# Softmax weights times values as plain float32 on two column halves, in a two-block transformer on one core

## The chip, the cores and the metric

The program runs on one core of one Trainium2 chip. Its engines run side by side and are held together by semaphores: TensorE (PE in the rows; its weight loads are PEld), VectorE (DVE), ScalarE (ACT), GpSimd (POOL) and SyncE (SP), which here issues the DMAs. The metric is the device time of one execution in microseconds, lower is better. The kernel before has a median of 2799.71 us over 3 runs (2798.59 to 2801.4). The profiled execution took 2796.16 us, and its span, from the first recorded instruction to the last, is 2794.4 us at a mean granted TensorE clock of 0.982 of full speed.

## The reference, cut to what matters

Two layers of one block and two layers of a second block follow one another on a sequence of 256 tokens of width 1024, in float32. Three places multiply softmax weights with values, and only these are changed. In the first block there are two attention branches, with 8 heads of value width 64 each: grouped (2 key/value heads shared by 4 query heads each) and latent (8 value heads of their own). The sequence x looks at 512 keys, the context sequence c at its own 256, and c is only computed in the first of the two layers:

```
def block(qi):
    s = jnp.einsum("bqkgd,btkd->bkgqt", qi, k).astype(jnp.float32)
    w = jax.nn.softmax(s, axis=-1).astype(v.dtype)
    return jnp.einsum("bkgqt,btkd->bqkgd", w, v)
```

In the second block a sparse attention with 8 heads in 2 groups adds three products of weights and values for each head: over 15 compressed blocks, over selected blocks and over a window. With 256 tokens the selected blocks and the window take in all earlier keys.

```
o_cmp = jnp.einsum('bghqc,bcgd->bqghd', p_cmp.astype(v_cmp.dtype), v_cmp)
o_slc = jnp.einsum('bghqk,bgqkd->bqghd', p_s.astype(vs.dtype), ...)
o_win = jnp.einsum('bghqk,bkgd->bqghd', p_w.astype(vwc.dtype), vwc)
```

All the rest (projections, a Fourier branch, gates, MLPs, gated linear attention, norms) is the same before and after.

## The kernel before, in words

Matrix products keep float32 accuracy by splitting each operand into a high and a low part of a shorter type (float32r, `F32R` in the code): h is a rounded copy written by ScalarE, l is the rest, subtracted by VectorE (`split`, L183 and L189). `mm3` (L196) then issues three matmuls, h·h, h·l and l·h. This holds for the streamed weights (`wr` is the raw tile, `wh` and `wl` the parts), for activations (tiles S and H) and, before the change, for softmax weights and values too. Transposes (`tr`, L201) and a few small products run in plain float32.

Attention goes unit by unit, a unit being one head and one tile of 128 queries. A unit has three steps. `scores` multiplies queries and keys into the PSUM tile `sc`, takes the row maximum (`Vcm`, VectorE), the exponential with its row sum (`ea`, ScalarE), the reciprocal and the product by it (VectorE). `turn` transposes the weights on TensorE into PSUM tile `tp`, 128 keys at a time, and splits them into `eh` and `el`. `apply` multiplies them with the values into another `tp` tile: for each 128 keys three matmuls with 64 value columns as the stationary operand and 128 queries moving, so that only 64 of the array's 128 columns are in use; the result, 64 rows by 128 queries, is split into the output activation (S).

The values are held as h and l pairs: `vg` (grouped, tiles H), `V` (latent, tiles S, made by `build_v`), `vsw` (sparse, H) and, for the compressed branch, `cmp["v"]` and the weights `eTc` (H).

`pipe` runs the steps of neighbouring units in turn: scores of unit n, turn of unit n-1, apply of unit n-2. `mix` puts other matrix products (gate and branch projections, modulation, gated linear attention's projections) between these steps: each step yields its estimated TensorE time, and for each such amount times a ratio (`RATIO`, 1.5, 1.2 and so on by stage) it draws steps of the other work; what is left of that runs behind. The framework then schedules each engine's instructions by a simulated timeline within the program's dependencies, and its buffers have fixed counts (`eh` and `el` 2 each, `ea` 3, PSUM `mm` 3, `sc` 2, `tp` 3). All weight DMAs go out from SyncE.

The three stages in the profiled execution: grouped and latent attention of the first layer from about 185 to 530 us, of the second from about 1030 to 1190 us, sparse attention from about 1690 to 1830 us and from about 2375 to 2510 us.

Of the kernel before, what the change touches and what calls it, by code (L numbers as in the profile page):

```python
# [21 lines left out]
P = 128  # L22
D = 1024
S = 256
# [3 lines left out]
BIG = 3e38  # L28
ALPHA = (2.0 * L) ** 0.25
# [119 lines left out]
class Builder:  # L149
# [543 lines left out]
    def attend(self, pairs, nk, vs, h, out, c0):  # L693
# [5 lines left out]
        st = {}  # L699

        def scores():
            sc = self.pt("sc")
            prs = pairs()
# [6 lines left out]
            e = st["e"] = self.t("ea", [P, nk])  # L710
# [5 lines left out]
        def turn():  # L716
            tp = self.pt("tp", [P, kt, P])
            for a in range(kt):
                self.tr(tp[:, a], st["e"][:, a * P:(a + 1) * P])
            st["w"] = [self.t("eh", [P, kt, P], F32R), self.t("el", [P, kt, P], F32R)]  # L720
            yield cost(kt, P)
            self.split(tp, *st["w"])

        def apply():
            eh, el = st["w"]
            po = self.pt("tp")
            for a in range(kt):
                self.mm3(po[:64, :P], vs(a), (eh[:, a], el[:, a]), a == 0, a == kt - 1)
            yield 0.056 * 3 * kt
            oh, ol = out.at(h // 2, c0, P)  # L730
            b = slice(64 * (h % 2), 64 * (h % 2) + 64)
            self.split(po[:64, :P], oh[b], ol[b])
        return scores, turn, apply

    def first_layer(self, l, X, hT, done):
# [21 lines left out]
        vg = [self.t("H", [P, 4, P], F32R) for _ in range(2)]  # L757
# [21 lines left out]
        def ev_kg(i, ps):  # L779
# [3 lines left out]
            self.split(ps[:, P:2 * P], vg[0][:, kt], vg[1][:, kt])  # L783
# [91 lines left out]
        def grouped(s, h, t):  # L875
            g, j = divmod(h, 4)
            gs = slice(64 * g, 64 * g + 64)
            nk = nkeys(s)
            return self.attend(lambda: [(qg[s][g][:, j, t * P:(t + 1) * P], k[:, :nk]) for k in kgT[g]], nk,
                               lambda a: (vg[0][:, a, gs], vg[1][:, a, gs]), h, OT["g"], OFF[s] + t * P)  # L880

        gqa = self.pipe([load_dft] + [fourier(s, g) for s in full for g in range(4)] +
                        [grouped(s, h, t) for s in full for h in range(8) for t in range(2)])
# [74 lines left out]
        def build_v(p):  # L958
            wv = self.load_w(A["w_uv"][l][:, p * P:(p + 2) * P], 2, 2 * P)
            V[p] = V[p + 1] = [self.t("S", [P, 4, 2 * P], F32R) for _ in range(2)]  # L960
            for a in range(0, 4, 2):
# [6 lines left out]
                self.split(ps, V[p][0][:, a:a + 2], V[p][1][:, a:a + 2])  # L968
# [32 lines left out]
        def latent(s, p, i, t):  # L1001
            nk = nkeys(s)
            c = (p % 2) * P + 64 * i
            def pairs():
# [3 lines left out]
            return self.attend(pairs, nk, lambda a: (V[p][0][:, a, c:c + 64], V[p][1][:, a, c:c + 64]),  # L1008
                               2 * p + i, OT["m"], OFF[s] + t * P)

        steps = [partial(build_v, 0), partial(build_k, 0)] + [partial(build_q, s, 0) for s in full]
        for p in range(4):
            for s in full:
                units = [latent(s, p, i, t) for i in range(2) for t in range(2)]
# [236 lines left out]
    def mix2(self, x, st, l, nxt):  # L1251
# [8 lines left out]
        vsw = [self.t("H", [P, 2, 2, P], F32R) for _ in range(2)]  # L1260
# [24 lines left out]
        def ev_kv2(i, ps):  # L1285
            self.split(ps[:, 0:P], vsw[0][:, i, 0], vsw[1][:, i, 0], scale=r[i])
            key_rows(ps[:, P:2 * P], i, 1)
            self.split(ps[:, 2 * P:3 * P], vsw[0][:, i, 1], vsw[1][:, i, 1], scale=r[i])
# [129 lines left out]
    def compress(self, l, kc, name, cmp):  # L1418
# [48 lines left out]
        else:  # L1467
# [18 lines left out]
            o = [self.t("H", [P, 2, 4, 64], F32R) for _ in range(2)]  # L1486
            self.split(z, *o)
        cmp[name] = o

    def nsa(self, qT, ksw, vsw, ga, cmp, OA):  # L1490
# [3 lines left out]
        eTc = [self.t("H", [P, 2, S], F32R) for _ in range(2)]  # L1494
# [37 lines left out]
        self.split(tp, *eTc)  # L1532
        yield cost(8, P)

        def unit(h, t):
            g, j = divmod(h, 4)
            gs = slice(64 * g, 64 * g + 64)
            o = slice(64 * (h % 2), 64 * (h % 2) + 64)
            nk = P * (t + 1)
            n = 2 * (t + 1)  # L1540
            st = {}

            def scores():
                sc = self.pt("sc", [P, 2, 256])
                j0 = 128 - 128 * t
                self.mm2(sc[:, :, :nk], qT[g][:, j // 2, j % 2, t * P:(t + 1) * P], [k[:, :, :nk] for k in ksw[g]])
# [4 lines left out]
                e = st["e"] = self.t("ea", [P, 2, nk])  # L1551
                for b in range(2):
                    nc.vector.tensor_tensor_reduce(e[:, b], sc[:, b, :nk], self.bias[g][:, j, j0:j0 + nk], -1.0, BIG,
# [7 lines left out]
                nc.vector.tensor_tensor(a_, a_, g3[:, h, 1:3], op=ALU.mult)  # L1561
# [3 lines left out]
            def turn():  # L1565
                tp = self.pt("tp", [P, 4, P])
                for a in range(n):
                    b, k = divmod(a, t + 1)
                    self.tr(tp[:, a], st["e"][:, b, k * P:(k + 1) * P])
                st["w"] = [self.t("eh", [P, n, P], F32R), self.t("el", [P, n, P], F32R)]  # L1570
                yield cost(n, P)
                self.split(tp[:, :n], *st["w"])

            def apply():
                eh, el = st["w"]
                ts = slice(t * P, (t + 1) * P)
                po = self.pt("tp")
                out = po[:64, :P]
                self.mm3(out, (cmp["v"][0][:, g, j], cmp["v"][1][:, g, j]),
                         (eTc[0][:, g, ts], eTc[1][:, g, ts]), True, False)  # L1580
# [3 lines left out]
                yield 0.056 * 3 * (n + 1)  # L1584
                oh, ol = OA.at(h // 2, t * P, P)
                self.split(out, oh[o], ol[o])
            return scores, turn, apply
# [223 lines left out]
```

## Time and profile before

| | |
|---|---|
| median of 3 runs | 2799.71 us |
| profiled execution | 2796.16 us |
| its span | 2794.4 us |
| granted TensorE clock, mean | 0.982 |
| PE busy | 2700.5 us, 97% of the span |
| PEld busy | 2377.2 us, 85% |
| DVE busy | 1925.0 us, 69% |
| ACT busy | 1479.7 us, 53% |
| POOL busy | 167.4 us, 6% |

How to read it: an engine's busy time is the union of its records. TensorE's matmuls are pipelined, and a record lasts from its start to its modelled end, so records overlap and their length is not what each costs; the cost of one is read from the distance between the starts of neighbours. In the chain of work that ended last PE holds 75% of the span, and "issue" (time in which the engine waited for nothing that the profile shows) another 15%.

### The profile page before, as it was taken

What the parts mean: (1) busy time and instruction counts of PE and PEld (TensorE: products, weight loads), DVE (VectorE), ACT (ScalarE), POOL (GpSimd) and SP (SyncE); (2) the same over time, 40 slices, a digit from 0 to 9 for tenths busy, and PEclk for the clock granted to TensorE, in tenths of its full rate; (3) what the DMA queues carried; (4) which work ended last, traced back from release to release, by engine and by line L of the source; (5) the groups of instructions that cost most, each with busy time, mean ns of one, the idle gap of its engine ahead of it and who ended that gap; (6) DMA issues with size and microseconds to landing.
All of it is one profiled execution on the core that took longest, in us unless ns stands there. A gap on an engine that the chain in (4) does not pass through costs nothing.

```text
span 2794.4 us, 45721 instructions
## 1 busy us (share of the span) xinstructions
PE 2700.5 (97%) x17359; PEld 2377.2 (85%) x17359; DVE 1925.0 (69%) x3754; ACT 1479.7 (53%) x2970; POOL 167.4 (6%) x304
## 2 busy tenths in 40 slices
PE   8999999999999999979989999999999998999998
PEld 4868878788777799968979987999999988889997
DVE  5676776587886788866675567867656656787664
ACT  6474564453344666655454456645444446665543
POOL 1200010100000210010000001100000000020000
PEclk9999999999999999989999999999999999999999
DMA  7251232465554333346555555446666655436664
GB/s 233 80 166 43 79 114 85 153 216 159 162 184 140 112 108 104 113 145 217 190 188 169 194 158 171 125 142 188 183 189 190 184 181 172 142 94 191 183 185 151
DMA packets 258610, 431.97 MB, mean 155 GB/s; under 512 B 18020, under 2 KB 89100, under 8 KB 258390
## 3 DMA queue, kind: packets, MB, share of 16 engines
q1 hardware_dynamic: 258390, 429.05, 49.6%
q8 instruction: 136, 2.23, 0.3%
q14 instruction: 84, 0.69, 0.1%
HBM read 425.75 MB, written 3.24 MB: 154 GB/s over the span
## 4 chain that ended last, share of the span: by engine, by line
PE 75%; issue 15%; DVE 4%; ACT 2%; DMA 2%; POOL 1%; SPq 0%; DVEq 0%; POOLq 0%; ACTq 0%
PE mm L196 62%; PE tp L196 3%; PE sc L196 3%; PE tp L201 3%; PE sc L705 2%; DVE wl L189 1%; DMA wr<-w_ada 1%; ACT wh L183 1%; PE sc L207 0%; DMA wr<-w_in 0%; DMA wr<-w_o 0%; ACT H L567 0%; POOL Var L233 0%; DVE S L629 0%; DVE S L214 0%
## 5 line engine op out<-in xcount | busy, mean ns | idle before, releaser
L196 PE MATMUL mm<-S,wh 128*128 128x256 f32 (+1 forms) x6112 | 1255.3, 303 | 3.6 <-ACT wh L183 1.3
L189 DVE TENSOR_TENSOR wl<-wr,wh 128x512 fp32r<-128x512 f32 (+2 forms) x1256 | 886.7, 739 | 499.5 <-ACT wh L183 494.8
L183 ACT ACTIVATE wh<-wr 128x512 fp32r<-128x512 f32 (+2 forms) x1256 | 780.1, 662 | 748.5 <-PE mm L196 385.1
L196 PEld LDWEIGHTS mm<-S,wh 128*128 128x128 f32 x6112 | 987.3, 191 | 51.5 <-ACT wh L183 2.8
L196 PE MATMUL mm<-S,wl 128*128 128x256 f32 (+1 forms) x3056 | 918.5, 303 | 2.0 <-DVE wl L189 2.0
L196 PE MATMUL mm<-wh,S 128*128 128x512 f32 (+4 forms) x2592 | 775.5, 378 | 11.7 <-ACT S L183 4.0
L196 PEld LDWEIGHTS mm<-S,wl 128*128 128x128 f32 x3056 | 583.1, 191 | 25.5 <-DVE wl L189 3.9
L196 PEld LDWEIGHTS mm<-wh,S 128*128 128x128 f32 x2592 | 478.5, 190 | 100.0 <-issue 7.0
L196 PE MATMUL mm<-wl,S 128*128 128x512 f32 (+4 forms) x1296 | 487.9, 377 | 0.4 <-DVE wl L189 0.4
L196 PEld LDWEIGHTS mm<-wl,S 128*128 128x128 f32 x1296 | 245.7, 190 | 42.6 <-DVE wl L189 1.2
L201 PE MATMUL tp<-cst,ea 128*128 128x128 f32 x632 | 103.9, 286 | 19.3 <-ACT ea L578 11.1
L495 DVE SCALAR_TENSOR_TENSOR H<-wr,cs,H 128x512 f32<-128x512 f32 x168 | 116.1, 747 | 0.0
L201 PEld LDWEIGHTS tp<-cst,ea 128*128 128x128 f32 x632 | 77.5, 146 | 32.4 <-ACT ea L578 13.0
L183 ACT ACTIVATE eh<-tp 128x512 fp32r<-128x512 f32 (+1 forms) x128 | 65.8, 515 | 58.4 <-PE tp L201 57.7
L189 DVE TENSOR_TENSOR el<-tp,eh 128x512 fp32r<-128x512 f32 (+1 forms) x128 | 74.7, 584 | 30.6 <-ACT eh L183 29.1
L196 PE MATMUL mm<-H,S 128*128 128x512 f32 x384 | 94.2, 392 | 0.3 <-DVE H L189 0.3
L183 ACT ACTIVATE S<-tp 64x128 fp32r<-64x128 f32 (+2 forms) x178 | 60.1, 344 | 58.7 <-PE tp L196 48.7
L196 PEld LDWEIGHTS mm<-H,S 128*128 128x128 f32 x384 | 71.5, 188 | 16.6 <-DVE S L629 0.9
L189 DVE TENSOR_TENSOR S<-tp,S 64x128 fp32r<-64x128 f32 (+2 forms) x178 | 66.3, 376 | 26.3 <-ACT S L183 23.7
L711 ACT ACTIVATE ea<-sc,Vcm 128x512 f32<-128x512 f32 (+1 forms) x96 | 59.0, 615 | 34.5 <-DVE Vcm L708 34.0
L183 ACT ACTIVATE S<-H 128x512 fp32r<-128x512 f32 x106 | 65.2, 621 | 12.4 <-DVE H L934 4.9
L708 DVE TENSOR_REDUCE Vcm<-sc 128x1 f32<-128x512 f32 (+1 forms) x96 | 56.8, 596 | 20.2 <-PE sc L705 19.4
(328 smaller groups left out, 2697.8 us busy)
## 6 DMA issues: line engine op xcount, KB each, us to landing
wr<-w_in SPq DMA_DIRECT2D x160, 512.0 KB
wr<-w SPq DMA_DIRECT2D x116, 512.0 KB
wr<-w_ada SPq DMA_DIRECT2D x96, 512.0 KB
wr<-ffn_w_gate SPq DMA_DIRECT2D x88, 512.0 KB
wr<-ffn_w_down SPq DMA_DIRECT2D x88, 512.0 KB
wr<-ffn_w_up SPq DMA_DIRECT2D x84, 512.0 KB
wr<-w_branch_gla SPq DMA_DIRECT2D x16, 512.0 KB
wr<-w_out SPq DMA_DIRECT2D x16, 512.0 KB
```

The source lines that it names most:

```text
L183: nc.scalar.activation(h, src, AF.Copy, scale=1.0 if scale is None else scale)
L189: (nc.gpsimd if le == "p" else nc.vector).tensor_tensor(l, src, h.bitcast(F32), op=ALU.subtract)
L196: self.nc.tensor.matmul(out, a[i], b[j], start=first and n == 0, stop=last and n == 2, skip_group_check=skip)
L201: self.nc.tensor.transpose(out, in_, self.ident[:n, :n])
L495: nc.vector.scalar_tensor_tensor(acc[j], raw[:, k], c, acc[j], op0=ALU.mult, op1=ALU.add)
L705: nc.tensor.matmul(sc[:, :nk], a, b, start=n == 0, stop=n == len(prs) - 1)
L708: nc.vector.tensor_reduce(nm, sc[:, :nk], axis=AX.X, op=ALU.max, negate=True)
L711: nc.scalar.activation(e, sc[:, :nk], AF.Exp, bias=nm, scale=1.0, accum_out=sm)
```

## The change

Softmax weights and values are no longer split in the three places. The values (`vg`, `V`, `vsw`, `cmp["v"]`) and the transposed weights (`ws`, `eTc`) are single float32 tiles, each written by one ScalarE copy. Two heads are handled together: the unit list now alternates between head 0 of a pair (scores, turn) and head 1 of the pair (scores, turn, apply), and `apply` serves both heads. It calls the new `col2`, which for each 128 keys issues one plain float32 matmul for head 0 into PSUM partitions 0 to 63 (columns 0 to 63 of the array) and one for head 1 into partitions 64 to 127 (columns 64 to 127). The result of both heads, 128 rows by 128 queries, is split once. Head 0's weights lie in the tiles `eh`, head 1's in `el`. `mix` is told 0.24 (`COL2`) for each pair of matmuls, where it was told 0.056 for each of the six before. In all 1344 matmuls of the split kind become 448 plain ones, in 224 pairs.

```diff
+COL2 = 0.24
...
+    def col2(self, out, terms, cost_):
+        for n, (a, b) in enumerate(terms):
+            for i in range(2):
+                self.nc.tensor.matmul(out[64 * i:64 * i + 64], a[i], b[i], start=n == 0, stop=n == len(terms) - 1,
+                                      tile_position=(0, 64 * i))
+        yield len(terms) * cost_
...
-        def turn():
+        def turn(i):
             tp = self.pt("tp", [P, kt, P])
             for a in range(kt):
-                self.tr(tp[:, a], st["e"][:, a * P:(a + 1) * P])
-            st["w"] = [self.t("eh", [P, kt, P], F32R), self.t("el", [P, kt, P], F32R)]
+                self.tr(tp[:, a], es[i][:, a * P:(a + 1) * P])
+            ws[i] = self.t(("eh", "el")[i], [P, kt, P])
             yield cost(kt, P)
-            self.split(tp, *st["w"])
+            nc.scalar.activation(ws[i], tp, AF.Copy)
 
         def apply():
-            eh, el = st["w"]
-            po = self.pt("tp")
-            for a in range(kt):
-                self.mm3(po[:64, :P], vs(a), (eh[:, a], el[:, a]), a == 0, a == kt - 1)
-            yield 0.056 * 3 * kt
-            oh, ol = out.at(h // 2, c0, P)
-            b = slice(64 * (h % 2), 64 * (h % 2) + 64)
-            self.split(po[:64, :P], oh[b], ol[b])
-        return scores, turn, apply
+            po = self.pt("tp")[:, :P]
+            yield from self.col2(po, [([vs(i, a) for i in range(2)], [ws[i][:, a] for i in range(2)])
+                                      for a in range(kt)], COL2)
+            oh, ol = out.at(hp, c0, P)
+            self.split(po, oh, ol)
+        return [(partial(scores, 0), partial(turn, 0)), (partial(scores, 1), partial(turn, 1), apply)]
...
-            self.split(ps[:, P:2 * P], vg[0][:, kt], vg[1][:, kt])
+            nc.scalar.activation(vg[:, kt], ps[:, P:2 * P], AF.Copy)
...
-                self.split(ps, V[p][0][:, a:a + 2], V[p][1][:, a:a + 2])
+                nc.scalar.activation(V[p][:, a:a + 2], ps, AF.Copy)
...
-            self.split(ps[:, 0:P], vsw[0][:, i, 0], vsw[1][:, i, 0], scale=r[i])
+            nc.scalar.activation(vsw[:, i, 0], ps[:, 0:P], AF.Copy, scale=r[i])
...
-        self.split(tp, *eTc)
+        nc.scalar.activation(eTc, tp, AF.Copy)
...
+                terms = [([cmp["v"][:, g, j + i] for i in range(2)], [eTc[:, g, t * P:(t + 1) * P]] * 2)]
                 for a in range(n):
                     b, k = divmod(a, t + 1)
-                    self.mm3(out, (vsw[0][:, k, b, gs], vsw[1][:, k, b, gs]), (eh[:, a], el[:, a]), False, a == n - 1)
+                    terms.append(([vsw[:, k, b, gs]] * 2, [ws[i][:, a] for i in range(2)]))
+                yield from self.col2(po, terms, COL2)
```

The instruction order on TensorE, in the grouped attention of the first layer, where the second `apply` of the stage begins. Before (`mm` rows are a gate projection of the other work, `H_502` and `H_503` the high and low part of the values, `eh` and `el` those of the weights):

```order
L196 MATMUL mm_2178<-S_96,wh_2297 128x512
L196 MATMUL mm_2178<-S_95,wl_2298 128x512
L196 MATMUL mm_2178<-S_97,wh_2297 128x512
L196 MATMUL tp_2042<-eh_2003,H_502 64x128
L196 MATMUL tp_2042<-el_2004,H_502 64x128
L196 MATMUL tp_2042<-eh_2003,H_503 64x128
```

The three last rows come four times in a row, once for each 128 keys. Now, at the same place (`eh` holds the weights of head 0, `el` those of head 1, `H_502` the values in one part):

```order
L197 MATMUL mm_2142<-S_95,wl_2234 128x512
L202 MATMUL tp_2088<-cst,ea_2033 128x128 x4
L699 MATMUL tp_2095<-eh_2014,H_502 64x128
L197 MATMUL mm_2143<-S_91,wh_2146 128x512
L197 MATMUL mm_2143<-S_92,wh_2146 128x512
L699 MATMUL tp_2095<-el_2043,H_502 64x128
```

Three rows for each 128 keys of one head have become two rows for both heads. Here two rows of other work have come between the two heads of the first pair; in the whole program the 448 matmuls stand in 81 uninterrupted runs in 64 PSUM tiles, before the 1344 stood in 131 runs in 128 tiles.

On VectorE, in the same stage, before (`el` is the low part of the weights, the output S is split for one head, 64 rows, at a time):

```order
L189 TENSOR_TENSOR S_1303<-tp_2212,S_1302 64x128
L189 TENSOR_TENSOR el_2244<-tp_2238,eh_2243 128x512
L189 TENSOR_TENSOR S_1303<-tp_2247,S_1302 64x128
L708 TENSOR_REDUCE Vcm_2332<-sc_2329 128x1
L189 TENSOR_TENSOR wl_2759<-wr_2756,wh_2758 128x1024
L708 TENSOR_REDUCE Vcm_2367<-sc_2364 128x1
L189 TENSOR_TENSOR el_2279<-tp_2273,eh_2278 128x512
```

And now:

```order
L190 TENSOR_TENSOR S_1298<-tp_2095,S_1297 128x128
L718 TENSOR_REDUCE Vcm_2127<-sc_2124 128x1
L723 RECIPROCAL Vcr_2132<-Vcs_2129 128x1
L724 TENSOR_SCALAR ea_2130<-ea_2130,Vcr_2132 128x512
L718 TENSOR_REDUCE Vcm_2189<-sc_2186 128x1
L190 TENSOR_TENSOR wl_2520<-wr_2517,wh_2519 128x1024
```

The rows that write `el` are gone, and one row writes the output of both heads.

## Rows read from the trace of the kernel before

**Rows 1.** The page: span, and busy time, share and instructions of PE

```profile
span 2794.4 us, 45721 instructions
...
PE 2700.5 (97%) x17359; PEld 2377.2 (85%) x17359; DVE 1925.0 (69%) x3754; ACT 1479.7 (53%) x2970; POOL 167.4 (6%) x304
```

**Rows 2.** Busy time by stretch: stretch, length, engines, clock, DMA share

```profile
core 0: us, PE busy (x) PEld busy (x) DVE busy (x) ACT busy (x) POOL busy (x), PEclk, DMA share, GB/s
...
185.00:325.00 140.00, 140.00 (x944) 120.74 (x943) 92.79 (x224) 74.97 (x182) 3.66 (x2) 1.00 0.20 57
...
1030.00:1190.00 160.00, 159.15 (x1428) 153.49 (x1427) 129.47 (x290) 102.60 (x241) 6.32 (x4) 1.00 0.35 105
...
1690.00:1830.00 140.00, 131.31 (x940) 118.09 (x940) 111.80 (x293) 86.59 (x210) 22.18 (x37) 0.94 0.44 131
```

**Rows 3.** Waits of PE, 1030:1190: who waited for whom, us, times, longest

```profile
PE tp L196 <- DVE el L189: 0.5, 1, 0.5
```

**Rows 4.** Groups of PE by form: operation, shapes, count | busy, mean ns

```profile
L196 PE MATMUL tp<-eh,H 128*64 128x128 f32 x512 | 61.5, 227 | 0.0
L196 PE MATMUL tp<-el,H 128*64 128x128 f32 x256 | 50.0, 224 | 0.0
L196 PE MATMUL tp<-eh,S 128*64 128x128 f32 x320 | 38.8, 229 | 0.1
...
L196 PE MATMUL tp<-el,S 128*64 128x128 f32 x160 | 31.2, 224 | 0.6 <-DVE el L189 0.6
...
L196 PE MATMUL tp<-H,H 128*64 128x128 f32 x96 | 12.4, 239 | 0.0
```

**Rows 5.** Timeline of PE, one apply of 12 matmuls: start, length, instruction

```profile
1061.04 0.22 PE L196 MATMUL tp<-eh,H 128*64 128x128 f32 x1
1061.10 0.22 PE L196 MATMUL tp<-el,H 128*64 128x128 f32 x1
...
1061.71 0.23 PE L196 MATMUL tp<-eh,H 128*64 128x128 f32 x1
1061.78 0.45 PE L196 MATMUL mm<-S,wh 128*128 128x256 f32 x2
```

**Rows 6.** The group of weight loads of 64 columns, by form

```profile
L196 PEld LDWEIGHTS tp<-eh,H 128*64 128x64 f32 x512 | 53.6, 137 | 0.6
```

**Rows 7.** Timeline, plain float32 of 512 columns moving: loads, then matmuls

```profile
529.00 0.09 PEld L527 LDWEIGHTS sc<-wr,cs 128*4 128x4 f32 x1 [0.34 <-issue]
529.43 0.09 PEld L527 LDWEIGHTS sc<-wr,cs 128*4 128x4 f32 x1 [0.34 <-issue]
...
528.57 3.60 PE L527 MATMUL sc<-wr,cs 128*4 128x512 f32 x8
532.10 5.76 PE L196 MATMUL mm<-H,S 128*128 128x512 f32 x24
```

**Rows 8.** Timeline of PE, plain float32 of 128 columns moving

```profile
1785.12 0.60 PE L1626 MATMUL sc<-cst,S 128*128 128x128 f32 x4
1785.48 0.42 PE L196 MATMUL tp<-H,H 128*64 128x128 f32 x3
1785.74 0.23 PE L196 MATMUL tp<-eh,H 128*64 128x128 f32 x1
```

**Rows 9.** The group of PE for that line, by form

```profile
L1626 PE MATMUL sc<-cst,S 128*128 128x128 f32 x32 | 5.0, 277 | 0.0
```

**Rows 10.** Groups of DVE by form: work of the weights' and outputs' split

```profile
L189 DVE TENSOR_TENSOR el<-tp,eh 128x512 fp32r<-128x512 f32 x80 | 54.7, 685 | 18.5 <-ACT eh L183 18.1
...
L189 DVE TENSOR_TENSOR S<-tp,S 64x128 fp32r<-64x128 f32 x128 | 35.9, 280 | 20.2 <-ACT S L183 17.7
...
L189 DVE TENSOR_TENSOR el<-tp,eh 128x256 fp32r<-128x256 f32 x48 | 20.0, 417 | 12.1 <-ACT eh L183 11.1
```

**Rows 11.** The ACT group of the outputs' split, by form

```profile
L183 ACT ACTIVATE S<-tp 64x128 fp32r<-64x128 f32 x128 | 34.4, 269 | 45.8 <-PE tp L196 43.9
```

More of the change, by code (lines that the diff above doesn't have):

```diff
@@ L756, in first_layer @@
         kgT = [[self.t("H", [P, 512], F32R) for _ in range(2)] for _ in range(2)]
-        vg = [self.t("H", [P, 4, P], F32R) for _ in range(2)]
+        vg = self.t("H", [P, 4, P])
         gkv = self.col("mla_kv_g", l)
@@ L1013, in first_layer @@
             for s in full:
-                units = [latent(s, p, i, t) for i in range(2) for t in range(2)]
+                units = [u for t in range(2) for u in latent(s, p, t)]
                 if p < 3:
@@ L1259, in mix2 @@
         ksw = [[self.t("H", [P, 2, S], F32R) for _ in range(2)] for _ in range(2)]
-        vsw = [self.t("H", [P, 2, 2, P], F32R) for _ in range(2)]
+        vsw = self.t("H", [P, 2, 2, P])
         ga = [None, None]
@@ L1485, in compress @@
                 nc.vector.tensor_copy(z[s_, :, a_], ps[s_, :P].rearrange("p (g d) -> p g d", g=2))
-            o = [self.t("H", [P, 2, 4, 64], F32R) for _ in range(2)]
-            self.split(z, *o)
+            o = z
         cmp[name] = o
@@ L1491, in nsa @@
         nc = self.nc
-        eTc = [self.t("H", [P, 2, S], F32R) for _ in range(2)]
+        eTc = self.t("H", [P, 2, S])
         raw = self.pt("tp", [P, 2, 2, P])
@@ L1568, in turn @@
                     b, k = divmod(a, t + 1)
-                    self.tr(tp[:, a], st["e"][:, b, k * P:(k + 1) * P])
-                st["w"] = [self.t("eh", [P, n, P], F32R), self.t("el", [P, n, P], F32R)]
+                    self.tr(tp[:, a], es[i][:, b, k * P:(k + 1) * P])
+                ws[i] = self.t(("eh", "el")[i], [P, n, P])
                 yield cost(n, P)
-                self.split(tp[:, :n], *st["w"])
+                nc.scalar.activation(ws[i], tp[:, :n], AF.Copy)
             def apply():
[L1575 to L1580, printed above, removed]
+                po = self.pt("tp")[:, :P]
+                terms = [([cmp["v"][:, g, j + i] for i in range(2)], [eTc[:, g, t * P:(t + 1) * P]] * 2)]
                 for a in range(n):
                     b, k = divmod(a, t + 1)
-                    self.mm3(out, (vsw[0][:, k, b, gs], vsw[1][:, k, b, gs]), (eh[:, a], el[:, a]), False, a == n - 1)
[L1584 to L1587, printed above, removed]
-        yield from self.pipe([unit(h, t) for h in range(8) for t in range(2)])
+                    terms.append(([vsw[:, k, b, gs]] * 2, [ws[i][:, a] for i in range(2)]))
+                yield from self.col2(po, terms, COL2)
+                oh, ol = OA.at(hp, t * P, P)
+                self.split(po, oh, ol)
+            return [(partial(scores, 0), partial(turn, 0)), (partial(scores, 1), partial(turn, 1), apply)]
+        yield from self.pipe([u for hp in range(4) for t in range(2) for u in units(hp, t)])
     def decays(self, l, alr, la):
```

52 lines of the change are left out of this document (25 added, 27 removed).

## The prediction

> **What bounds the kernel now.** I read the page first: PE is busy for 97% of the span and VectorE for 69% [rows 1]. That is a mean over stages, so I next read the busy time by stretch, at the three places that the change touches. In the first layer's attention PE is busy for all of 140 us, and VectorE for 92.79 of them; in the second layer's for 159.15 of 160, VectorE for 129.47; in the sparse attention for 131.31 of 140, VectorE for 111.80 [rows 2]. Then the waits: in the second layer's attention TensorE waited once for `el`, the low part of the weights, and that for 0.5 us [rows 3]. So in these stages TensorE's own work sets the time, and what counts is what the changed matmuls cost there. VectorE's and ScalarE's work lies beside it.
>
> **What is removed on TensorE.** The groups by form give 512, 256, 320, 160 and 96 matmuls of 64 stationary columns and 128 moving ones [rows 4], 1344 in all, three for each 128 keys of a head. Their mean of some 225 ns is no price, since records overlap. The timeline has twelve of them from 1061.04 to 1061.78, where the next product starts [rows 5]: 0.74 us, or 0.0617 us each, with the load of each one's weights included. That load's record is 137 ns long [rows 6], so loads are already hidden behind the matmuls before them. Removed: 1344 x 0.0617 = 82.9 us.
>
> **What is added on TensorE.** 448 plain float32 matmuls of 64 stationary and 128 moving columns, in 224 pairs. No plain one of 64 columns stands in the trace of before, so I price it by two others. The line of the 128 x 128 running sums, L1626, is reached 16 times (four heads, two tiles, two layers) and has 32 rows [rows 9]: a plain float32 matmul makes two rows. With 512 columns moving, the loads between such rows lie 0.43 us apart, and only the first 0.09 us of that is the load [rows 7]; a quarter of the columns makes 0.43 / 4 = 0.1075 us for a row of 128. The running sums agree: four rows and three matmuls of the split kind take from 1785.12 to 1785.74 [rows 8], and (0.62 - 3 x 0.0617) / 4 = 0.109. So one plain matmul costs 0.215 us, and a pair costs 0.43 us if the two run one behind the other, against 6 x 0.0617 = 0.37 us for the six that it replaces.
>
> All depends, then, on whether the two halves of the columns work at the same time, which nothing in the trace of before shows. Bounds: one behind the other, 448 x 0.215 = 96.3 us, which is 13.4 us more than was removed; wholly side by side, 224 x 0.215 = 48.2 us, or 34.7 us less. I take the case between them that follows if matmuls start in the order in which they stand, as all rows of the timeline do: head 0's second row then runs beside head 1's first, head 1's second beside the first of head 0's next matmul, and a run of n pairs lasts 2n + 1 rows, because in its first and its last row only one half has work. The matmuls stand in 81 runs, so 448 + 81 = 529 rows x 0.1075 = 56.9 us. TensorE gains 82.9 - 56.9 = 26.0 us. For the loads: a pair needs four of 64 columns, and before such a load came every 0.0617 us with a matmul, so four take at most 0.25 us, which is about what the pair takes anyway (56.9 / 224 = 0.254). They don't change the sum, but they leave no reserve.
>
> The Trainium skill, on its page TensorE: Matmul & The Clock Gate, section Measured speedup vs the span model, reports 2.38 times for three tiles side by side in the columns. An estimate from it for two tiles, at the same efficiency, is 1.59 times: 96.3 / 1.59 = 60.6 us, by which the sum would be 22 us instead of 26. No run so far shows it here.
>
> **What goes on VectorE and ScalarE.** The subtractions for `el` take 54.7 + 20.0 us [rows 10] and go; of the 128 output splits half stay, with twice the partitions and the same row length, which saves half of 35.9 us on VectorE [rows 10] and half of 34.4 on ScalarE [rows 11]. That is 92.7 us off VectorE and 17.2 off ScalarE, beside a few rows for the values. I count them at nothing: where TensorE is busy all the time, it hides them already. Bounds: nothing lost, since the engines only get lighter; at most what TensorE idles in these stages, and that is 8.7 us in the first sparse stretch [rows 2] and next to none in the other two. Most of the sparse idle time stands before the units begin, where only the copy of `eTc` gets shorter, so I take 0. `apply` still waits for one ScalarE copy, no longer for a subtraction behind it; behind a waiting `apply` on TensorE stand the next products of other work, as before. What `mix` puts between the steps shrinks with the yields (0.24 for a pair, where six times 0.056 was told), and what is not drawn there runs behind, as dense TensorE work. This moves work and adds none. The DMAs stay the same and have room (share 0.20 to 0.44 in these stages [rows 2]).
>
> **Sum.** 2796.2 us, the profiled execution (its span and 1.8 us around it), less 26.0 is 2770.2. The median of the runs is 3.5 us above the profiled execution, which makes 2773.7, or 2774.
>
> **The rivals.**
> 1. *The halves don't overlap.* Plain float32 holds the array for both heads in turn; a pair costs 0.43 us and the kernel becomes slower by 13.4 us: 2813. For it: nothing in this trace shows two matmuls side by side. Against: the halves write different PSUM partitions and have their own weights, so they share only the order of issue. It decides from 0.37 us for a pair.
> 2. *They overlap by half.* The second half of the array waits for its load, as four loads in a pair leave no reserve: midway between 96.3 and 56.9, 76.6 us, a gain of 6.3: 2793. Against: the pitch of 0.0617 us for load and matmul together [rows 5].
> 3. *More is gained.* No lost row at the ends of runs (34.7 us), and some of the idle time of the sparse stages goes with the lighter VectorE, say 4 us: 2761. For it: VectorE at 111.80 of 140 in the sparse stretch [rows 2].
> 4. *Attention's chain comes to the surface.* With less TensorE work between two steps, the chain of maximum, exponential and product is waited for; 0.5 us (the one wait of [rows 3]) at each of the 64 `apply` steps is 32 us, which turns the gain into a loss of 6: 2806. Against: hardly a wait in these stages now, and VectorE gets lighter by more than TensorE.
> 5. *Loads are exposed.* Each of the 896 rows waits for its own load: 0.137 [rows 6] + 0.1075 us, 219 us in all, 136 more than before: 2936. Against: the loads before were hidden at the same rows of the array.
>
> The Trainium skill, on the same page, section The mechanism, says that a weight load overlaps with matmuls in flight only where the row group differs; both halves here use all rows, so by that rule it would be rival 5. The trace disagrees in the form that it has: loads with 137 ns records at a pitch of 61.7 ns [rows 5, 6], all on the same rows, so that rival gets little.
>
> **How the numbers follow.** Forecast 68%, no overlap 8%, half overlap 10%, more gained 7%, the chain 4%, exposed loads 3%. A measurement of this kernel can tell 0.2%, about 5.6 us, from no change. Faster: the forecast, the third case and 7 of the 10 in a hundred of the second, 0.82. Same: the rest of the second, 0.03. Slower: the first, fourth and fifth, 0.15. The range runs from the third case (2761) to a little above half overlap (2796), which leaves out the first, fourth and fifth case and a few of the hundred at its edges, under two in ten.
>
> **What would show it.** In the profile after, two rows for each plain matmul, 896 in all, and a run of four pairs from its first start to the next foreign start in about 9 x 0.1075 = 0.97 us (1.72 if the halves don't overlap), where two heads took 1.48 before. The `el<-tp` subtractions gone, VectorE's busy time near 1830 us, and TensorE still busy nearly all the time in the three stages, each shorter by its share: 160 of the 448 groups of three lie in the grouped attention, 160 in the latent, 128 in the sparse one. It would be wrong if the runs of pairs take over 1.48 us, or if the gain on the pairs appears while TensorE waits for `ea` or the weights' copy in their place.

## The result and the profile after

The changed kernel takes 2757.16 us (median of 4 runs, 2752.65 to 2762.43), the kernel before, on the same chip, 2800.39 us: a ratio of 0.9847 [0.9827, 0.9867]. That is 43.2 us less, where 26 were forecast, and 4 us below the range. The page of the profiled execution (span; busy time, share and instructions of each engine), against [rows 1]:

```profile
span 2750.9 us, 44582 instructions
...
PE 2678.2 (97%) x16911; PEld 2330.8 (85%) x16911; DVE 1837.9 (67%) x3534; ACT 1460.4 (53%) x2904; POOL 167.3 (6%) x304
```

TensorE is busy 22.3 us less, but the span is 43.5 us shorter: about half of the gain is time in which TensorE did nothing. Three stretches in the stages of [rows 2], with the same columns (not the same work: the second holds 1082 matmuls, the one of [rows 2] 1428):

```profile
185.00:325.00 140.00, 140.00 (x849) 112.95 (x848) 73.31 (x176) 71.45 (x169) 2.57 (x2) 1.00 0.19 54
1020.00:1150.00 130.00, 129.86 (x1082) 120.85 (x1081) 89.73 (x207) 83.38 (x193) 6.21 (x4) 1.00 0.36 105
1675.00:1800.00 125.00, 121.97 (x847) 106.58 (x848) 100.68 (x265) 83.42 (x200) 25.67 (x40) 0.97 0.49 146
```

The first two are as dense as before; the sparse one idles 3 us where it idled 8.7, at a granted clock of 0.97 instead of 0.94.

**The pairs.** An `apply` of four pairs in the timeline of PE (start, length, instruction), against [rows 5]:

```profile
237.99 0.32 PE L699 MATMUL tp<-eh,H 128*64 128x128 f32 x1
237.99 0.32 PE L699 MATMUL tp<-el,H 128*64 128x128 f32 x1
238.15 0.27 PE L699 MATMUL tp<-eh,H 128*64 128x128 f32 x1
238.15 0.27 PE L699 MATMUL tp<-el,H 128*64 128x128 f32 x1
238.26 0.27 PE L699 MATMUL tp<-eh,H 128*64 128x128 f32 x1
238.26 0.27 PE L699 MATMUL tp<-el,H 128*64 128x128 f32 x1
...
238.81 0.27 PE L699 MATMUL tp<-el,H 128*64 128x128 f32 x1
239.01 0.44 PE L202 MATMUL tp<-cst,ea 128*128 128x128 f32 x2
```

Both heads' rows (`eh` is head 0, `el` head 1) start at the same moment, and in the middle the next two follow 0.11 us later, so the halves work wholly side by side. The first row takes 0.16 us and the last one 0.20 until the transpose behind it starts. Four pairs last 1.02 us, close to the 0.97 forecast, though by another way than forecast. One group of these rows, and one of their weight loads, by form:

```profile
L699 PE MATMUL tp<-el,S 128*64 128x128 f32 x160 | 22.6, 280 | 0.4 <-ACT el L732 0.4
```

```profile
L699 PEld LDWEIGHTS tp<-el,H 128*64 128x64 f32 x256 | 27.5, 136 | 2.5 <-ACT wh L184 0.7 <-ACT eh L732 0.4 <-issue 0.4
```

In all five groups TensorE waited 0.4 us, for one copy, and a load's record is as long as before [rows 6].

**Where the time went.** From the starts and ends of all TensorE rows and the clock's record I split each span into four parts: the time in which PE is not busy (span less PE busy on the page); what its rows took longer because they stood at 1.2 GHz (half of that time); the value products and transposes, each counted from its start to the next start, at full clock; all other products.

| us | before | after | difference |
|---|---|---|---|
| PE not busy | 93.9 | 72.7 | -21.2 |
| longer at half clock | 34.1 | 22.9 | -11.2 |
| value products | 86.0 | 65.3 | -20.7 |
| transposes | 79.4 | 87.7 | +8.3 |
| other products | 2501.0 | 2502.3 | +1.3 |
| span | 2794.4 | 2750.9 | -43.5 |

TensorE's own work gives only 11.1 us (20.7 less 8.3 and 1.3). Waits and clock give 32.4, which the forecast had at nothing. Two waits of PE in the kernel before (who waited for whom: us, times, longest):

```profile
PE tp L201 <- DVE H L768: 6.6, 2, 3.6
...
PE tp L201 <- DVE H L1527: 5.7, 2, 2.8
```

After the change neither line waits. The longer of the first two, in the timeline of before (in brackets the wait and what ended it), and ten microseconds around it by engine, clock and DMA, as in [rows 2]:

```profile
1012.94 0.29 PE L196 MATMUL mm<-wh,S 128*128 128x288 f32 x1
1016.79 0.41 PE L201 MATMUL tp<-cst,H 128*128 128x128 f32 x2 [3.55 <-DVE H L768]
```

```profile
1013.00:1023.00 10.00, 6.45 (x42) 6.20 (x42) 6.98 (x21) 5.33 (x17) 3.19 (x8) 0.83 0.55 160
```

The transposes wait for a norm chain whose last step is VectorE's (L768), and behind the wait the clock is at its lower level. The same place after the change, timeline and window:

```profile
1005.08 0.29 PE L197 MATMUL mm<-wh,S 128*128 128x288 f32 x1
1005.21 0.38 PE L202 MATMUL tp<-cst,H 128*128 128x128 f32 x2
```

```profile
1000.00:1010.00 10.00, 10.00 (x82) 10.00 (x81) 7.19 (x22) 7.66 (x22) 4.56 (x8) 1.00 0.29 82
```

PE is busy all the time, and the clock is full. On TensorE the transposes stand directly behind the same product in both. What differs is ScalarE, which begins the norm chain with a square (L239, after the change L240). Before, then after:

```profile
1011.34 1.15 ACT L183 ACTIVATE wh<-wr 128x512 fp32r<-128x512 f32 x2 [0.34 <-PE mm L196]
...
1012.81 1.15 ACT L183 ACTIVATE wh<-wr 128x512 fp32r<-128x512 f32 x2
1013.98 0.38 ACT L239 ACTIVATE H<-mm 128x256 f32<-128x256 f32 x1
```

```profile
1002.46 0.38 ACT L240 ACTIVATE H<-mm 128x256 f32<-128x256 f32 x1
...
1003.42 2.35 ACT L184 ACTIVATE wh<-wr 128x512 fp32r<-128x512 f32 x4
```

Before, four casts of streamed weights (2.3 us) stand in front of the square; after, they stand behind it. VectorE had subtractions of the same weights in front of its part of the chain before, and yet it waited at the end for GpSimd, the chain's middle step:

```profile
1016.16 0.48 DVE L765 TENSOR_SCALAR H<-mm,Vr 128x256 f32<-128x256 f32 x1 [0.46 <-POOL Vr L233]
```

At the second wait (L1527, before the transposes of the compressed softmax) the orders differ on TensorE itself: before, the attention's own two groups of `sc` products follow directly on one another, after the change 16 rows of other products (`mm`, from 1709.95 us) stand between them, of which the last is shown. Before, then after:

```profile
1728.67 1.22 PE L207 MATMUL sc<-H,S 128*128 128x512 f32 x4 [0.55 <-DVE Vcm L1553]
1732.73 1.09 PE L201 MATMUL tp<-cst,H 128*128 128x128 f32 x4 [2.83 <-DVE H L1527]
```

```profile
1713.37 0.39 PE L197 MATMUL mm<-wh,S 128*128 128x512 f32 x1
1713.59 0.85 PE L208 MATMUL sc<-H,S 128*128 128x512 f32 x4
1714.53 0.63 PE L202 MATMUL tp<-cst,H 128*128 128x128 f32 x4
```

So the engines have another order of instructions after the change, at the first wait in a place whose code the change doesn't touch. The experiments ask why.

### The profile page after: what moved, and what is told of

The parts are those of the page before. It is cut to its first block, busy times and chain, and to the rows that moved or that the text cites. A ratio compares the mean times of both kernels' runs of the same rounds, so it can differ in the third digit from the quotient of the medians.

```text
span 2750.9 us, 44582 instructions
## 1 busy us (share of the span) xinstructions
PE 2678.2 (97%) x16911; PEld 2330.8 (85%) x16911; DVE 1837.9 (67%) x3534; ACT 1460.4 (53%) x2904; POOL 167.3 (6%) x304
## 4 chain that ended last, share of the span: by engine, by line
PE 76%; issue 15%; DVE 3%; DMA 3%; ACT 2%; POOL 1%; SPq 0%; DVEq 0%; POOLq 0%; ACTq 0%
PE mm L197 62%; PE sc L197 4%; PE tp L202 3%; PE tp L699 2%; PE sc L715 2%; DMA wr<-w_ada 1%; DVE wl L190 1%; PE tp L197 1%; DMA wr<-w_o 0%; DMA wr<-w 0%; PE sc L208 0%; ACT wh L184 0%; ACT H L568 0%; POOL Vdr L234 0%; POOL Var L234 0%
## 5 line engine op out<-in xcount | busy, mean ns | idle before, releaser
L197 PEld LDWEIGHTS mm<-S,wl 128*128 128x128 f32 x3056 | 581.1, 191 | 22.9 <-DVE wl L190 1.6
L190 DVE TENSOR_TENSOR S<-tp,S 128x128 fp32r<-128x128 f32 (+2 forms) x114 | 48.8, 433 | 42.8 <-ACT S L184 42.4
L184 ACT ACTIVATE S<-tp 128x128 fp32r<-128x128 f32 (+2 forms) x114 | 43.3, 390 | 44.4 <-PE tp L699 32.2
L190 DVE TENSOR_TENSOR S<-H,S 128x512 fp32r<-128x512 f32 x86 | 58.6, 686 | 10.0 <-ACT S L184 9.5
L197 PE MATMUL sc<-wh,H 128*30 128x256 f32 (+2 forms) x240 | 55.7, 311 | 7.6 <-ACT H L184 5.6
```

The lines of the kernel that those rows point to most:

```text
L184: nc.scalar.activation(h, src, AF.Copy, scale=1.0 if scale is None else scale)
L190: (nc.gpsimd if le == "p" else nc.vector).tensor_tensor(l, src, h.bitcast(F32), op=ALU.subtract)
L197: self.nc.tensor.matmul(out, a[i], b[j], start=first and n == 0, stop=last and n == 2, skip_group_check=skip)
```

## The experiments

Columns: median and ratio to the kernel before with its interval; then parts of the profiled span as above (value products and transposes together: 165.4 us before, 153.0 after), and VectorE's busy time. The groups of runs stand on several chips, and each ratio is to the kernel before on the same chip, whose median there lay between 2798.3 and 2800.4 us; so a difference of two or three us between runs of different groups says nothing.

| run | us | ratio | PE not busy | half clock | values + transposes | DVE busy |
|---|---|---|---|---|---|---|
| after | 2757.16 | 0.9847 [0.9827, 0.9867] | 72.7 | 22.9 | 153.0 | 1837.9 |
| e1 one half | 2800.28 | 1.0006 [0.9996, 1.0016] | 72.9 | 23.7 | 198.0 | 1856.3 |
| e2 subtraction kept | 2769.75 | 0.9896 [0.9881, 0.9911] | 84.0 | 26.2 | 151.9 | 1892.7 |
| e3 old pace | 2753.39 | 0.9839 [0.9824, 0.9853] | 73.3 | 20.2 | 152.3 | 1840.0 |
| e4 tiles held | 2754.68 | 0.9840 [0.9818, 0.9862] | 74.1 | 22.9 | 153.1 | 1840.1 |
| e5 all VectorE work | 2784.29 | 0.9952 [0.9933, 0.9971] | 92.1 | 36.4 | 150.4 | 1921.3 |
| e6 first block only | 2780.55 | 0.9938 [0.9921, 0.9954] | 85.6 | 34.3 | 157.9 | 1857.8 |
| e7 sparse only | 2769.97 | 0.9905 [0.9886, 0.9924] | 80.4 | 28.7 | 160.5 | 1906.4 |
| e8 pairs' order alone | 2800.88 | 1.0005 [0.9994, 1.0016] | 93.1 | 41.4 | 166.1 | 1923.9 |
| e9 pipeline order | 2764.65 | 0.9881 [0.9866, 0.9895] | 72.5 | 18.5 | 160.1 | 1838.7 |
| e10 long runs | 2754.94 | 0.9844 [0.9827, 0.9860] | 73.4 | 22.2 | 153.4 | 1836.9 |
| e11 scale on ScalarE | 2762.77 | 0.9873 [0.9858, 0.9888] | 79.3 | 25.3 | 152.1 | 1785.2 |
| e12 e10 and e11 | 2768.39 | 0.9891 [0.9876, 0.9906] | 79.6 | 22.7 | 154.9 | 1777.0 |
| e13 heavy in place | 2759.63 | 0.9859 [0.9845, 0.9874] | 85.3 | 20.2 | 147.8 | 1916.4 |
| e14 heavy, after's order | 2767.45 | 0.9884 [0.9862, 0.9907] | 84.0 | 29.7 | 153.1 | 1921.5 |
| e15 light, e13's order | 2760.02 | 0.9856 [0.9840, 0.9873] | 84.6 | 24.1 | 147.4 | 1833.4 |
| e16 tiles alone | 2778.56 | 0.9925 [0.9908, 0.9942] | 93.3 | 24.8 | 153.4 | 1849.9 |
| e17 tiles and time | 2786.05 | 0.9956 [0.9942, 0.9970] | 95.8 | 28.2 | 152.0 | 1915.5 |
| e18 light, e17's order | 2780.17 | 0.9930 [0.9914, 0.9945] | 95.7 | 27.0 | 151.5 | 1837.4 |

**e1: do the halves carry the gain on TensorE?** Both heads' products go into the same 64 columns, one behind the other.

```diff
-                self.nc.tensor.matmul(out[64 * i:64 * i + 64], a[i], b[i], ..., tile_position=(0, 64 * i))
+                self.nc.tensor.matmul(out[:64, P * i:P * i + P], a[i], b[i], ...)
```

> The changed kernel, but the plain float32 matmuls of both heads go to the same 64 columns of the array (two regions of one PSUM tile), and the output is split per head again. If the halves worked side by side and that is what gained, a pair now costs four rows of 0.1075 us instead of two: the value matmuls take 96 us on TensorE instead of 67, and the kernel takes about 2787 to 2800 us. If the gain came from elsewhere (VectorE, order), it stays within 10 us of the changed kernel's 2757.

The timeline of PE in e1, from the middle of an `apply` (two rows of one matmul in each line):

```profile
238.19 0.38 PE L699 MATMUL tp<-eh,H 128*64 128x128 f32 x2
238.41 0.38 PE L699 MATMUL tp<-el,H 128*64 128x128 f32 x2
238.63 0.38 PE L699 MATMUL tp<-eh,H 128*64 128x128 f32 x2
```

The two heads alternate at 0.22 us for two rows, 0.11 us each, as the prediction priced a row. The value products take 45.2 us longer than side by side (110.5 against 65.3), and the whole gain is gone. Waits and clock stay as after the change, so they are a matter of their own.

**e2 to e4: three causes for the waits.** e2 adds a subtraction behind each copy of the turned weights, into a tile that nobody reads. e3 tells `mix` 0.336 for a pair, as six times 0.056 was. e4 holds three H tiles through the sparse attention.

```diff
             nc.scalar.activation(ws[i], tp, AF.Copy)
+            nc.vector.tensor_tensor(self.t("H", [P, kt, P]), tp, ws[i], op=ALU.subtract)     # e2
...
-COL2 = 0.24
+COL2 = 0.336     # e3
...
+        self.hold = [self.t("H", [P, 512])]     # e4, and two more; all read after the last apply
+        nc.gpsimd.memset(self.hold[0][:, :4], 0.0)
```

> The changed kernel, with the subtraction for the low part of each transposed weight tile left on VectorE (75 us in all), into a tile that nobody reads. Theory 1 (the 17 us beyond the matmuls came because a lighter VectorE lets TensorE wait less in the sparse stages): about 2770 to 2777 us, with TensorE's idle time near the 82 us of before. Theory 2 (they came from another order of instructions) and theory 3 (from buffers set free): within 6 us of 2757.

> The changed kernel, with the pace told to mix as before (0.336 for a pair instead of 0.24), so that other products are drawn between the attention steps as they were before the change. If the vanished waits come from the pace, 2768 to 2777 us with the waits back; if not, within 6 us of 2757, with the waits of the sparse stages still gone.

> The changed kernel, with three tiles of the H pool held through the sparse attention, as many as the low parts of its values and weights held before. Theory 3 (freed H buffers let other work start earlier, which fills the waits of the sparse stages): about 2770 to 2777 us, with waits back near the compressed softmax and in the gated linear attention behind it. Theories 1 and 2: within 6 us of 2757, unless the order moves.

Neither the pace nor the freed H tiles is the cause: e3 and e4 keep the whole gain. e2 brings back 14.6 of the 32.4 us (not busy 11.3, half clock 3.3), so I held the lighter VectorE for the cause.

**e5 to e8: VectorE's load against the order.** e5 puts all the VectorE work back as subtractions into H and Q tiles and splits the outputs per head. e6 and e7 make the change in one place alone. e8 only queues the units of before by pairs of heads.

```diff
+            nc.vector.tensor_tensor(self.t("H", [P, kt, P]), tp, ws[i], op=ALU.subtract)     # e5; likewise vg, V, vsw, eTc
-            self.split(po, oh, ol)
+            for i in range(2):
+                b = slice(64 * i, 64 * i + 64)
+                self.split(po[b], oh[b], ol[b])
```

> The changed kernel, with all the VectorE work that the change removed put back as subtractions into tiles that nobody reads (after each turn, for V, vg, vsw and the transposed compressed weights, and the split of each output made per head). Theory 1, the lighter VectorE is what took away 32.5 us of waits and half-clock time on TensorE: both come back, idle plus half-clock extra near 124 us as before instead of 91, and the time is near 2786 us, at least 2780. Theory 2, the other order of the instructions took them away and the subtraction's 14.6 us are all that VectorE carries: it stays near e2, 2766 to 2773 us.

> The change in the grouped and latent attention of the first layer type alone (320 of the 448 plain products); the sparse attention stays as before. If the gain is TensorE's own work, 320/448 of the 11.1 us net, about 8 us, comes from here: 2792 us. If the waits and the half-clock time matter as the trace of the changed kernel has them (the gaps that went lie in the stretches of the sparse and the gated linear attention too), this part alone leaves the gaps of 2.8 us before the compressed softmax's transposes where they are: 2775 to 2785 us.

> The change in the sparse attention alone (128 of the 448 plain products); grouped and latent attention stay as before. TensorE's own work gives 128/448 of 11.1, about 3 us: 2796 us. Theory 1 (lighter VectorE in the stretch itself): the two gaps of 2.8 us before the compressed softmax's transposes and the half clock behind them go as well, another 12 us: 2784 us. The gains of e6 and e7 should add to that of the whole change, 43 us, within 5 us if each stretch's waits are its own.

> The kernel before, with its attention units queued by pairs of heads in the order that the change gives them; the arithmetic, the splits and the number of instructions are as before. Theory 2 (the order alone removes the waits): 15 to 30 us faster, 2770 to 2785 us. Theory 1: within 5 us of before, 2795 to 2805 us, and idle plus half-clock extra still about 120 us.

e5 came out as theory 1 had it: not busy and half clock back at 128.5 us (128.0 before). e6 and e7 together gain 46.8 us against the 43 of the whole, as if each stretch's waits were its own; e7, with 18.6 us off VectorE, gains more than e6 with 67, and 14 us more than I had expected of it, which theory 1 doesn't explain. In e6 the wait before the compressed softmax's transposes still stands as in before, now at L1534:

```profile
PE tp L202 <- DVE H L1534: 5.7, 2, 2.8
```

The pairs' order alone does nothing. But e5 changed two things that I had not kept apart. The framework writes each engine's order by a simulated timeline, so VectorE work that is added also rewrites the other engines' orders; and it took tiles from the pools, whose first writers are bound to the program's order. The last six runs take these apart.

**e9 to e12: fewer runs, less VectorE.** e9 takes the pipeline's steps as scores, apply, turn. e10, on e9, puts both query tiles of a pair of heads into one `apply`. e11 moves the scaling by 1/sum to ScalarE. e12 is e10 with e11.

```diff
-            for k in range(3):
+            for k in (0, 2, 1):     # e9, e10, e12
...
+            for t in range(2):     # e10, e12: in apply
+                yield from self.col2(po[:, t * P:t * P + P], ..., COL2, t == 0, t == 1)
...
-            nc.vector.tensor_scalar(e, e, rs, None, op0=ALU.mult)
+            nc.scalar.activation(e, e, AF.Copy, scale=rs)     # e11, e12
```

> The changed kernel with the three steps of the attention pipeline taken in the order scores, apply, turn. It is the control for e10, which needs that order. Both theories expect little: 2750 to 2765 us.

> The changed kernel with both query tiles of a pair of heads in one apply, so that the plain float32 products stand in about half as many runs, twice as long; the products are the same 896 rows. If entering and leaving a run costs about 0.25 us (0.16 before the first row and 0.20 behind the last, against 0.03 and 0.06 in the kernel before), some 40 runs fewer give 10 us: 2743 to 2750 us, with the value rows and the transposes beside them 8 to 11 us shorter. If the cost hangs on the rows or on each 128-column accumulation and not on the run, nothing: within 4 us of e9.

> The changed kernel with the softmax weights' scaling by 1/sum moved from VectorE to ScalarE (96 + 64 instructions, some 60 us of VectorE's time). If VectorE's load is what sets TensorE's small waits, relief goes on: 83 us off VectorE gave 32.5 us of waits and half-clock time, so 60 us give up to 20 us more; 2737 to 2752 us. Rival: ScalarE now waits for VectorE's reciprocal in the middle of each softmax, with the casts of the weights queued behind; then the casts come late and it is slower than the changed kernel, 2760 to 2780 us.

> e10 and e11 together. If the two gains are TensorE's switches on one side and waits on the other, they add: e10 plus what e11 gives against the changed kernel, within 5 us.

e9's order breaks the value products into 108 uninterrupted runs instead of 81, and they, the transposes and the other products together take 15.3 us longer (the other products 2510.5); e10 has 76 runs and takes 12.4 us less than e9 (others 2504.8), 0.39 us for each run. That fits a cost that hangs on the run, though the two orders differ in more than the runs. My expectation for e10 was wrong in its base: against the changed kernel it saves only 5 runs, and no time. e11 takes 53 us off VectorE and is 5.6 us slower; whether that is ScalarE's wait for the reciprocal or the order that came of it, this run doesn't tell. e12 is slower still; the gains don't add.

**e13 to e15: the same load, two orders.** e13's 218 subtractions write in place into the PSUM tile just copied out, so no pool tile is taken, and no instruction of another engine is added. e14 and e15 bind the order of every engine by dependencies without a semaphore, from a table of the other kernel's order.

```diff
+            self.idle_sub(tp, ws[i])     # e13, e14: tp -= ws; likewise the outputs' 64 rows, vg, V, vsw, eTc
...
+        ins = [i for i in nc.cur_bb.bb.instructions if str(i.engine) == "EngineType." + e and i.name not in DUM]
+        run = [ins[k] for k in np.cumsum(d)]     # e14, e15, e18: d is the table
+        for a, b in zip(run, run[1:]):
+            tc.add_manual_dep(b, a.name, mybir.DependencyInfo(mybir.DependencyClass.NoSync, ...))
```

> The changed kernel with 218 more subtractions on VectorE that nobody reads, in place on the PSUM tiles just copied out (turns, V, vg, vsw, compressed weights, and 64 rows of each output); PE, ScalarE, SyncE and GpSimd have the changed kernel's instructions, ordered anew by the framework's simulated timeline. As e5: near 2784 us (2776 to 2790), idle plus half-clock time on TensorE near 124 us.

> e13's VectorE work, with the order of all other instructions on all five engines bound to that of the changed kernel. Theory A, VectorE's load acts on the chip: it stays at e13's time, 2776 to 2790 us. Theory B, it acts through the order that the simulated timeline writes: it falls to the changed kernel's, 2755 to 2765 us. About half way, near 2770: both.

> The changed kernel's own instructions, bound on all five engines to the order of e13 (without its extra subtractions). Theory A: it stays at the changed kernel's 2757 us (2752 to 2762). Theory B: it rises to e13's, 2776 to 2790 us, and the gap of 3 us before the product sc<-eh,H in the sparse attention is back.

e13 refutes theory 1. Its VectorE is as busy as before:

```profile
PE 2672.5 (97%) x16911; PEld 2329.4 (84%) x16911; DVE 1916.4 (69%) x3752; ACT 1461.3 (53%) x2904; POOL 175.9 (6%) x304
```

and it takes 2759.63 us, 2.5 more than the changed kernel. e15, with the same order and without the load, takes the same: in that order VectorE's 83 us cost nothing. They aren't free in every order: in the changed kernel's own (e14) they cost some 10 us, though its interval is wide. e13 waits 12.6 us more (85.3) and gets about 8 of them back by fewer runs (72) and less time at half clock. The times that I had set for e14 and e15 went by a slow e13 and no longer part the theories; what e14 and e15 show is read from their own differences.

**e16 to e18: the tiles, and the order that comes of them.**

```diff
+            nc.vector.tensor_tensor(self.t("H", [P, kt, P])[:, 0, :1], (tp)[:, 0, :1], (ws[i])[:, 0, :1], op=ALU.subtract)     # e16; likewise the other places
+            nc.vector.tensor_tensor(self.t("H", [P, kt, P]), tp, ws[i], op=ALU.subtract)     # e17; likewise the other places
```

> The changed kernel with the same 218 extra subtractions as e13, but each of one column only (some 0.06 us instead of 0.28 to 0.69), and written into H and Q tiles allotted as in e5. Theory C, the tiles of the shared pools (their places, allotted in a fixed order) hold other work back: 2775 to 2786 us. Theory D, it needs VectorE's time as well: within 5 us of the changed kernel, 2753 to 2763 us.

> As e16 with the subtractions at their full width, without e5's split of the outputs per head. If tiles and time together are what e5 shows: 2778 to 2788 us. If the split per head (64 more ScalarE copies, two readers of the outputs) carries it: at most 2768 us.

> The changed kernel's own instructions, without any extra work or tile, bound on all five engines to the order that the builder wrote for e17. If e17's loss lies in the order: e17's time within 5 us. If it lies in the extra work and tiles on the chip: the changed kernel's 2757 us within 5 us.

In e16 VectorE has next to nothing to do for it (its group by form):

```profile
L733 DVE TENSOR_TENSOR H<-tp,eh 128x1 f32<-128x1 f32 x48 | 7.3, 153 | 13.4 <-ACT eh L732 12.9
```

and yet 21.4 us are lost. e18 settles how: it has the changed kernel's instructions and nothing else, no tile and no subtraction more, only e17's order, and loses 23.0 us. PE is idle for 95.7 us, as in e17 (95.8) and in before (93.9). The first wait of before is back at its place, with the casts in front of the square again and the half clock behind it (waits, then timelines of PE and ScalarE, then window):

```profile
PE tp L205 <- DVE H L778: 5.4, 2, 3.8
```

```profile
1015.16 0.29 PE L200 MATMUL mm<-wh,S 128*128 128x288 f32 x1
1019.23 0.66 PE L205 MATMUL tp<-cst,H 128*128 128x128 f32 x2 [3.77 <-DVE H L778]
```

```profile
1015.25 1.15 ACT L187 ACTIVATE wh<-wr 128x512 fp32r<-128x512 f32 x2
1016.42 0.39 ACT L243 ACTIVATE H<-mm 128x256 f32<-128x256 f32 x1
```

```profile
1015.00:1025.00 10.00, 6.23 (x41) 6.02 (x40) 7.36 (x21) 5.30 (x17) 3.25 (x8) 0.83 0.57 159
```

So the order in which the builder writes the instructions is worth over 20 us by itself, and added tiles are enough to change it. On the chip e17's tiles and VectorE time add 5.9 us to that, a little more than the 5 us within which I had called e17's loss one of order. The sum of e18's idle time is that of before, its parts only in part: the 5.7 us before the compressed softmax's transposes aren't back, and of the 11.2 us at half clock only 4.1 are.

No version beat the changed kernel by more than its interval; e3 and e4 came nearest.

## Why the prediction was wrong, step by step

1. **TensorE is the bound.** Right: it is 97% busy after as before, and nothing took its place (rival 4): the `el<-tp` subtractions are gone, and PE waits 0.4 us in all for the weights' copy.
2. **Removed, 82.9 us.** Near enough: from start to next start the value products of before take 86.0 us.
3. **Added, 56.9 us.** This term was mis-sized, by two errors of opposite sign. The halves overlap wholly: where the two heads stand together, both heads' rows start together and no end row is lost, as rival 3 had it. 448 pairs of rows at 0.109 us make 48.8 us. 72 of the 896 rows start alone, nearly all where other work stands between the two heads; that makes 36 steps more, 3.9 us. But a run of plain float32 products costs about 0.3 us to enter and leave, which the forecast didn't have. At full clock the transpose row before a run lasts 0.202 us, where one between transposes lasts 0.109; the run's first row lasts 0.160 and its last 0.203, against 0.109 in between; the transpose row behind it lasts 0.165. Together that is 0.29 us more than four such rows. In all the products cost 74.9 us (86.0 less 11.1), 22.2 more than the rows alone, over 81 runs 0.27 us each. The yardstick that I had set, 0.97 us for four pairs, was met (1.02) without showing it, since half of the cost stands outside these 1.02 us, in the transposes on either side. Net 11.1 us instead of 26.0.
4. **VectorE and ScalarE relief, counted at nothing.** As a statement on load this holds in e13's order (e13, e15); in the changed kernel's own the load cost some 10 us (e14). What failed is the step behind it: that where TensorE is busy in the three stages, all else stays. The waits that went stand partly outside them, where a chain of norm or softmax was waited for: at the wait of 3.55 us ScalarE had four weight casts in front of the chain, and before the compressed softmax's transposes TensorE had no other product in between. In all 21.2 us of waits and 11.2 of half clock went. The front had said that the order comes from a simulated timeline; the prediction took the order of the other work as given.
5. **The rivals.** No overlap and half overlap fell (e1 is what no overlap costs). Exposed loads fell: the pitch of 0.11 us is shorter than a load's record of 0.136 us. Rival 3 was nearest, with 2761, and its two parts were the right ones, but that its sum came near is luck: the rows gave 11.1 us instead of 34.7, and waits and clock 32.4 instead of 4.

With the measured terms, 2796.2 - 11.1 - 32.4 = 2752.7 us, which is the profiled execution after the change (2752.65); the terms are parts of the two spans, so they have to close and prove nothing more.

**What stays open.** e18 shows that order alone can cost what before lost. It isn't shown that the wait before the compressed softmax's transposes, which e18 didn't bring back, went by the order alone. Nor is it shown which part of the change made the builder write the better order: not the pairs' order alone (e8), not the pace (e3), not the H tiles of the sparse attention (e4), and hardly VectorE's shorter entries in the simulation, since e13, where they are as long as before, got an order as good. Left are the fewer tiles elsewhere, to which e16 points, and the four units that `eh` and `el` now serve where they served two. Before's order can't be bound onto the changed kernel, whose instructions differ.

## What to carry to other kernels

Where a builder orders the instructions by a simulation, every edit is also a new order, worth here over 20 us each way: list the waits of the whole program before and after, not only of the stages that were edited, follow each to the engine that began the chain (here the casts in front of a norm were ScalarE's), and bind the order in one experiment before a cause on the chip is believed. A dummy that takes a tile from a shared pool is no pure load; in place it cost 2.5 us, in a tile 29. Price a change of the kind of matmul by its runs as well as its rows, and keep the runs few and long.

## What the runs showed of the hardware

- Two plain float32 products in the two halves of the columns run side by side without loss: same start, 0.109 us a row for both, as for one of them alone in e1 (0.109).
- Entering and leaving a run of such products costs about 0.3 us, in the halves and in e1 (first row 0.160, last 0.203 before a transpose) alike, so it doesn't come from the second position. The 64-column products of the split kind before had no such cost: behind a transpose the last transpose row and the first row of the run took 0.028 and 0.141 us, together what the two take inside their own runs (0.109 and 0.060); behind a product of the split kind the first row took 0.060, and the last row 0.061. The Trainium skill, on its page TensorEngine Tiling (Array Packing), section Key Properties, says that changing the tiling mode drains TensorE. The runs agree for the plain products, with 0.3 us for both changes; by the same rule the products of before, of 64 columns too, should have paid it, and didn't. The Trainium skill, on its page PSUM — Partial Sum Buffer, section The four PSUM rules, mentions in passing that float32r matmuls force all column groups, which would be a reason; no run here shows it.
- Behind the wait of 3.55 us above, the granted clock fell to its lower level, 1.2 GHz, for 3.4 us (0.83 as the mean of the ten). It didn't behind every such wait: behind one of 3.03 us that ended 149 us into the span of before it stayed at its upper level, 2.4 GHz. In all 102.9 us of the span before stood at the lower level, 69.2 after. The second price of a wait was half as large as the wait (11.2 beside 21.2 us).
